# FFN up-projection tiles: three 256-column matmuls per weight tile, or one of 512 and one of 256 columns with the halves added afterwards

## Chip, cores and metric

The kernel runs on one core of a Trainium2 chip. The metric is the device time of one execution in microseconds (us); the time before is the median of three runs. Engines are named as in the profile: PE (TensorE, matmuls), PEld (its weight loads), DVE (VectorE), ACT (ScalarE), SP (the queue that issues the DMAs).

## Reference

Two decoder layers on a sequence of 256 tokens with 1024 channels, float32. Layer 0 is FFN, pool/SSD mixer, FFN; layer 1 is FFN, latent attention, FFN. Every sub-layer takes a normed and modulated input h. The part that the change touches is the FFN, which occurs four times:

```
def swiglu(h, w13, w2):
    a, b = jnp.split(h @ w13, 2, axis=-1)
    return (jax.nn.silu(a) * b) @ w2
```

h is 256 x 1024, w13 is 1024 x 5632 (2816 columns for a, 2816 for b), w2 is 2816 x 1024. The four FFNs are called FFN0 and FFN1 (layer 0), FFN2 and FFN3 (layer 1) below. The vectors that scale, shift and gate each sub-layer come from another product, c @ mod_w, spread over the kernel.

## The kernel before

Channels lie on the 128 partitions and the 256 tokens along the free dimension. Matmuls run in a reduced float32 format, so every float32 operand is split into a high part (rounded) and a low part (the rest), and a product is the sum of three: weight low x input high, weight high x input low, weight high x input high.

**Weights.** SP loads blocks of 16 weight tiles (128 x 128 each, 1 MB) into `raw` buffers. Half a block, a piece of 8 tiles, is rounded by ACT into `wh` (L222), and DVE subtracts to get `wl` (L223). The function `take()` hands out pieces in the order in which the matmuls use them and writes the preparation of a piece into the program four pieces ahead; `wh` and `wl` have five buffers each, so a piece can be prepared only when the tile five pieces earlier has been used. Between the weight blocks stand blocks of mod_w, two DVE instructions each (L210), which multiply and sum for the vectors of later sub-layers. FFN0 has one such block for nearly every weight block, FFN1 and FFN2 one for every second.

**An FFN** has two stages. In the a/b stage each of 22 column tiles j makes a pair: a_j and b_j, each 8 steps over the 1024 channels (one piece per tile). Then ACT computes s = silu(a) (L589), DVE g = b * s (L590), and `split` rounds g on ACT (L314) and takes the rest on DVE (L315), giving the high and low halves of column tile j. In the f stage eight output tiles f_d run over all 22 column tiles of g, and DVE adds each to x through the gate (L446, two instructions); from the new x, `chunk` makes the next sub-layer's input parts `uh` (ACT, L375) and `ul` (DVE, L376). The next sub-layer begins with matmuls named `u_...` that use these parts one channel tile after another, the last tile last.

**Two forms of a step.** The f stage and the output projections use `mm2`: the input lies as high and low half side by side (512 columns), `wh` meets both in one matmul, and `wl` meets the high half in a second one that adds onto one half of the result. The two halves of the result are added later (in the f stage by the two L446). The a/b stage uses `mm3` through `lin`: three matmuls of 256 columns onto one 256-column result. The input `hx` already lies side by side.

**What is not touched.** The first 8 pairs of FFN0 come from a special start (tiles `n`), and the first 3 pairs of FFN1, FFN2 and FFN3 from `norm.open` (tiles `u_a`, `u_b`). So `lin` makes 14 pairs in FFN0 (j = 8 to 21) and 19 in each other FFN (j = 3 to 21): 71 pairs, 142 tiles.

The order of each engine's instructions is fixed when the program is built, by a scheduler with its own estimates; on the chip each engine goes through its list strictly in order.

Of the kernel before, what the change touches and what calls it, by code (L numbers as in the profile page):

```python
# [13 lines left out]
AF = mybir.ActivationFunctionType  # L14
ALU = mybir.AluOpType
# [4 lines left out]
S = 256  # L20
NC = D // P
# [40 lines left out]
def trunk(ctx, tc, xT, c_row, pos, kc, cols, rows, mod_w, w13s, w13, w2, win_a, wdt,  # L62
          pool_w, wout_a, win_m, wkr, wkv, wq, wo, out):
    nc = tc.nc
    V, A, T = nc.vector, nc.scalar, nc.tensor
# [9 lines left out]
    def ps(name):  # L75
        return pp.tile([P, 512], F32, tag="ps", name=name)
# [3 lines left out]
    def slab(q, name, dt, shape):  # L80
        n = int(np.prod(shape))
        t = ap_.tile([P, n], dt, tag=f"s{q}", name=name)
        if len(shape) == 1:
            return t
        names = "abc"[: len(shape)]
        spec = f"p ({' '.join(names)}) -> p {' '.join(names)}"
        return t.rearrange(spec, **dict(zip(names, shape)))

    def tmp(name):
        return tp.tile([P, S], F32, tag="t", name=name)  # L90
# [154 lines left out]
    def take(m=1):  # L245
        if cur["off"] == 0:
            while len(pieces) < cur["piece"] + state["look"] and process_half():
                pass
        wh, wl, n = pieces[cur["piece"]]
        o = cur["off"]  # L250
        cur["off"] += m
        assert cur["off"] <= n
        if cur["off"] == n:
            cur["piece"] += 1
            cur["off"] = 0
        return wh[:, o * P : (o + m) * P], wl[:, o * P : (o + m) * P]

    def mm3(pt, w, xh, xl, first, last):
        wh, wl = w
        T.matmul(pt, wl, xh, start=first, stop=False)  # L260
        T.matmul(pt, wh, xl, start=False, stop=False)  # L261
        T.matmul(pt, wh, xh, start=False, stop=last)  # L262

    def mm2(pt, w, x, first, last):
        wh, wl = w
        T.matmul(pt, wh, x, start=first, stop=False)  # L266
        T.matmul(pt[:, S:], wl, x[:, 0], start=False, stop=last)  # L267
# [28 lines left out]
    def prep_gate(l, sub):  # L296
        i = l * 3 + sub
        m, b = mod_col(l, 3 * sub + 2)
        V.tensor_tensor(out=gt_t[:, i], in0=m, in1=b, op=ALU.add)
        if sub != 1:  # L300
            V.tensor_scalar(out=gt_t[:, i], in0=gt_t[:, i], scalar1=0.5, scalar2=None, op0=ALU.mult)
        return gt_t[:, i]
# [3 lines left out]
    hx = cp.tile([P, NC, 2, S], F32R, name="hx")  # L306
# [6 lines left out]
    def split(dh, dl, src):  # L313
        A.copy(dh, src)  # L314
        V.tensor_tensor(out=dl, in0=src, in1=dh.bitcast(F32), op=ALU.subtract)  # L315
# [37 lines left out]
    def warm_sqrt(name):  # L353
        d = sp.tile([P, 1], F32, tag="wsq", name=f"wsq_{name}", bufs=1)
        A.activation(d, eps_t, AF.Sqrt)
# [74 lines left out]
    def lin(name, xh, xl, nk=NC):  # L430
        pt = ps(name)
        for k in range(nk):
            mm3(pt[:, :S], take(), xh(k), xl(k), k == 0, k == nk - 1)
        return pt

    def lin2(name, x, nk):
        pt = ps(name)
        for k in range(nk):
            mm2(pt, take(), x(k), k == 0, k == nk - 1)
        return pt  # L440

    hhk, hlk = (lambda k: hh[:, k]), (lambda k: hl[:, k])

    def residual(pt, d, gate, nxt):
        for e in range(2):
            V.scalar_tensor_tensor(out=xt[:, d], in0=pt[:, e * S : (e + 1) * S], scalar=gate[:, d : d + 1],  # L446
                                   in1=xt[:, d], op0=ALU.mult, op1=ALU.add)
        nxt.chunk(d)
# [109 lines left out]
    def ffn(norm, l, sub, make_next, opened=()):  # L558
        gt = [slab(q, f"g{l}{sub}_{q}", F32R, [2, 2, S]) for q in range(NSLAB)]

        def gx(j):
            return gt[j // 2][:, j % 2]

        for j in range(NJ):
            s = tmp(f"s{l}{sub}{j}")
            g = tmp(f"g{l}{sub}{j}")
            if not opened and j < NU:
                pa, pb = norm.open((f"a{j}", f"b{j}"))
                if j == 0:
                    norm.finish()  # L570
                r = norm.r
                ba = sp.tile([P, 1], F32, tag="ub", name="ba")
                V.tensor_copy(ba, pa[:, S : S + 1])
                ta, tb = tmp("ta"), tmp("tb")
                V.tensor_tensor(out=ta, in0=pa[:, :S], in1=r, op=ALU.mult)
                A.activation(s, ta, AF.Silu, bias=ba[:, 0:1])
                V.tensor_tensor(out=tb, in0=pb[:, :S], in1=r, op=ALU.mult)
                V.scalar_tensor_tensor(out=g, in0=tb, scalar=pb[:, S : S + 1], in1=s,
                                       op0=ALU.add, op1=ALU.mult)
                for c in range(8):  # L580
                    if c * NU // 8 == j:
                        norm.h(c)
            else:
                if 2 * j < len(opened):
                    pa, pb = opened[2 * j : 2 * j + 2]
                else:
                    pa = lin(f"a{j}", hhk, hlk)
                    pb = lin(f"b{j}", hhk, hlk)
                A.activation(s, pa[:, :S], AF.Silu)  # L589
                V.tensor_tensor(out=g, in0=pb[:, :S], in1=s, op=ALU.mult)  # L590
            split(gx(j)[:, 0], gx(j)[:, 1], g)
        gate = prep_gate(l, sub)
        nxt = make_next()
        if (l, sub) == (1, 0):
            rope_tables()
        warm_sqrt(f"f{l}{sub}")
        for d in range(NC):
            pt = lin2(f"f{d}", gx, NJ)
            residual(pt, d, gate, nxt)
        return nxt  # L600
# [294 lines left out]
    def rope_tables():  # L895
        ang = tmp("ang")
        posi = tp.tile([P, S], I32, tag="t", name="posi")
        nc.sync.dma_start(posi, pos.partition_broadcast(P))
        V.tensor_copy(ang, posi)
        V.tensor_scalar(out=ang, in0=ang, scalar1=kct[:, KC_INV : KC_INV + 1], scalar2=None, op0=ALU.mult)  # L900
        for dst, shift in ((sin_t, 0.0), (cos_t, 0.25)):
            n = tmp("angn")
            t = tmp("angt")
            V.tensor_scalar(out=n, in0=ang, scalar1=float(1.0 / TWO_PI), scalar2=shift, op0=ALU.mult, op1=ALU.add)
            V.tensor_scalar(out=n, in0=n, scalar1=MAGIC, scalar2=None, op0=ALU.add)
            V.tensor_scalar(out=n, in0=n, scalar1=-MAGIC, scalar2=None, op0=ALU.add)
            V.scalar_tensor_tensor(out=t, in0=n, scalar=-C1, in1=ang, op0=ALU.mult, op1=ALU.add)
            V.scalar_tensor_tensor(out=t, in0=n, scalar=-C2, in1=t, op0=ALU.mult, op1=ALU.add)
            V.scalar_tensor_tensor(out=t, in0=n, scalar=-C3, in1=t, op0=ALU.mult, op1=ALU.add)
            if shift:  # L910
                V.tensor_scalar(out=t, in0=t, scalar1=float(np.pi / 2), scalar2=None, op0=ALU.add)
            V.tensor_scalar(out=t, in0=t, scalar1=PI_IN, scalar2=-PI_IN, op0=ALU.min, op1=ALU.max)
            A.activation(dst, t, AF.Sin)
# [269 lines left out]
    n = Norm(0, 0, scaled=False)  # L1183
    with tc.manual_schedule(engines={mybir.EngineType.PE, mybir.EngineType.DVE, mybir.EngineType.Activation}):
        pts = first_pairs(n)
    state["pin"] = True
    n = ffn(n, 0, 0, lambda: Norm(0, 1), pts)
    n = mixer_ab(n, 0, lambda: Norm(0, 2))
    n = ffn(n, 0, 2, lambda: Norm(1, 0))
    n = ffn(n, 1, 0, lambda: Norm(1, 1))  # L1190
    n = mixer_mla(n, 1, lambda: Norm(1, 2))
    n = ffn(n, 1, 2, Final)
# [144 lines left out]
```

## Time and profile before

| what | value |
|---|---|
| median of three runs | 1041.67 us (1041.18 to 1043.35) |
| profiled execution: its time, its span | 1042.6 us, 1040.8 us |
| busy in the span: PE, PEld, DVE, ACT | 1022.4, 957.7, 844.2, 576.4 us |
| granted TensorE clock, mean over the span | 0.993 |
| DMA, mean | 245 GB/s |

The span is the stretch that the trace covers; the execution's own time is 1.8 us longer. A busy PE row counts matmuls whose ends are modelled, so the pace of PE is read from start to start of successive matmuls and not from the duration of one. A name in brackets behind an instruction's idle time is what ended that wait.

### The profile page before, as it was taken

The page shows a single profiled execution, that of the slowest core. Times are in us where ns is not written, and L with a number is a line of the kernel's source. Part 1 is how long each engine was busy: PE and PEld are TensorE (multiplying, and loading weights), DVE is VectorE, ACT ScalarE, POOL GpSimd, SP SyncE. Part 2 cuts the span into 40 slices and gives each one's busy share as a digit, 9 for nine tenths or more (in the row PEclk, how much of TensorE's full clock was granted, in tenths as well). Part 3 has the DMA queues.
Part 4 walks back from the last instruction along what each step waited for, and adds up shares of the span by engine and source line. Part 5 has one row for each costly group of instructions (what it writes and reads, how often), then busy time and mean ns, then how long its engine had stood idle before and what let it go on. Part 6 is the DMA issues. An engine that isn't in the chain of part 4 may idle for free.

```text
span 1040.8 us, 18493 instructions
## 1 busy us (share of the span) xinstructions
PE 1022.4 (98%) x7436; PEld 957.7 (92%) x7436; DVE 844.2 (81%) x1523; ACT 576.4 (55%) x982; POOL 0.2 (0%) x4
## 2 busy tenths in 40 slices
PE   9899999999999999999999999999999999999997
PEld 7899998899878999998899999989988799999986
DVE  6888989999999887778879777899888688666553
ACT  3474453468795654445456444454678665444542
POOL 0000000000000000000000000000000000000000
PEclk9899999999999999999999999999999999999999
DMA  9988988977534477778766777798643246656501
GB/s 352 395 306 330 364 300 340 346 276 266 202 143 154 170 285 281 248 283 326 283 237 228 270 289 273 244 356 310 240 174 115 77 162 246 241 207 240 174 30 41
DMA packets 38648, 255.06 MB, mean 245 GB/s; under 512 B 4241, under 2 KB 6817, under 8 KB 8738
## 3 DMA queue, kind: packets, MB, share of 16 engines
q1 hardware_dynamic: 38562, 253.88, 66.6%
q8 instruction: 58, 0.95, 0.4%
q14 instruction: 28, 0.23, 0.1%
HBM read 252.79 MB, written 1.06 MB: 244 GB/s over the span
## 4 chain that ended last, share of the span: by engine, by line
PE 87%; DVE 7%; ACT 3%; DMA 1%; issue 1%; SPq 0%; DVEq 0%; ACTq 0%
PE f L266 15%; PE f L267 8%; PE a L260 7%; PE b L261 7%; PE b L260 7%; PE b L262 7%; PE a L262 7%; PE a L261 7%; PE o L266 4%; DVE wl L223 3%; DVE raw L210 2%; PE o L267 2%; PE n L522 1%; PE s L1074 1%; DMA raw<-in_w13s 1%; PE u_a L260 1%
## 5 line engine op out<-in xcount | busy, mean ns | idle before, releaser
L223 DVE TENSOR_TENSOR wl<-raw,wh 128x1024 fp32r<-128x1024 f32 x327 | 396.7, 1220 | 123.9 <-ACT wh L222 116.5
L222 ACT CAST wh<-raw 128x1024 fp32r<-128x1024 f32 x327 | 338.8, 1047 | 220.9 <-issue 92.9
L266 PE MATMUL f<-g,wh 128*128 128x512 f32 x704 | 248.9, 399 | 0.0
L267 PE MATMUL f<-g,wl 128*128 128x256 f32 x704 | 197.7, 281 | 0.0
L210 DVE SCALAR_TENSOR_TENSOR raw<-raw,c_bc 128x1024 f32<-128x1024 f32 x144 | 173.2, 1218 | 0.8 <-DMA raw<-in_mod_w 0.7
L266 PEld LDWEIGHTS f<-g,wh 128*128 128x128 f32 x704 | 132.3, 188 | 32.8
L260 PE MATMUL a<-hx,wl 128*128 128x256 f32 x568 | 160.8, 283 | 0.0
L261 PE MATMUL b<-hx,wh 128*128 128x256 f32 x568 | 160.7, 283 | 0.0
L262 PE MATMUL b<-hx,wh 128*128 128x256 f32 x568 | 160.7, 283 | 0.0
L260 PE MATMUL b<-hx,wl 128*128 128x256 f32 x568 | 160.7, 283 | 0.0
L262 PE MATMUL a<-hx,wh 128*128 128x256 f32 x568 | 160.6, 283 | 0.0
L261 PE MATMUL a<-hx,wh 128*128 128x256 f32 x568 | 160.5, 283 | 0.0
L267 PEld LDWEIGHTS f<-g,wl 128*128 128x128 f32 x704 | 133.0, 189 | 0.0
L260 PEld LDWEIGHTS a<-hx,wl 128*128 128x128 f32 x568 | 109.0, 192 | 0.6 <-ACT hx L400 0.6
L261 PEld LDWEIGHTS b<-hx,wh 128*128 128x128 f32 x568 | 109.1, 192 | 0.0
L262 PEld LDWEIGHTS b<-hx,wh 128*128 128x128 f32 x568 | 109.1, 192 | 0.0
L260 PEld LDWEIGHTS b<-hx,wl 128*128 128x128 f32 x568 | 109.0, 192 | 0.0
L262 PEld LDWEIGHTS a<-hx,wh 128*128 128x128 f32 x568 | 109.0, 192 | 0.0
L261 PEld LDWEIGHTS a<-hx,wh 128*128 128x128 f32 x568 | 108.9, 192 | 0.0
L589 ACT ACTIVATE s<-a 128x256 f32<-128x256 f32 x71 | 27.3, 384 | 88.5 <-PE a L262 88.5
L314 ACT CAST g<-g 128x256 fp32r<-128x256 f32 x88 | 35.3, 404 | 28.6 <-DVE g L590 19.8
L266 PE MATMUL o<-hx,wh 128*128 128x512 f32 x128 | 47.2, 410 | 0.7 <-DVE hx L315 0.7
(397 smaller groups left out, 1701.2 us busy)
## 6 DMA issues: line engine op xcount, KB each, us to landing
raw<-in_w SPq DMA_DIRECT2D x124, 1024.0 KB, 5.0
raw<-in_mod_w SPq DMA_DIRECT2D x70, 1024.0 KB, 5.3
raw<-in_win_a SPq DMA_DIRECT2D x12, 1024.0 KB, 7.1
raw<-in_w13s SPq DMA_DIRECT2D x7, 1024.0 KB, 11.1
raw<-in_wout_a SPq DMA_DIRECT2D x6, 1024.0 KB, 5.5
raw<-in_wq SPq DMA_DIRECT2D x5, 1024.0 KB, 4.8
raw<-in_win_m SPq DMA_DIRECT2D x4, 1024.0 KB, 5.0
raw<-in_wo SPq DMA_DIRECT2D x4, 1024.0 KB, 5.5
```

What stands on the lines that cost most here:

```text
L210: V.scalar_tensor_tensor(out=sl, in0=sl, scalar=1.0, in1=c_bc, op0=ALU.mult, op1=ALU.mult, accum_out=modc[:, c0 : c0 + 1])
L222: A.copy(wh[:, :n], src)
L223: V.tensor_tensor(out=wl[:, :n], in0=src, in1=wh[:, :n].bitcast(F32), op=ALU.subtract)
L260: T.matmul(pt, wl, xh, start=first, stop=False)
L261: T.matmul(pt, wh, xl, start=False, stop=False)
L262: T.matmul(pt, wh, xh, start=False, stop=last)
L266: T.matmul(pt, wh, x, start=first, stop=False)
L267: T.matmul(pt[:, S:], wl, x[:, 0], start=False, stop=last)
L314: A.copy(dh, src)
L522: T.matmul(tile_of(m), w, x[:, k], start=k == 0 and m % 2 == 0 and w is wl, stop=k == NC - 1 and w is wh and x is hh, skip_group_check=True)
L589: A.activation(s, pa[:, :S], AF.Silu)
L1074: T.matmul(pts[e][:, lo : lo + n], q[:, lo : lo + P], kk[:, 0:n], start=True, stop=False)
```

## The change

The a and b tiles that `lin` made are now made by `lin2`, with `mm2`: per step one 512-column matmul of `wh` with both halves of `hx`, and one 256-column matmul of `wl` with the high half, whose product lands on the second half of the result. The two halves have to be added before silu and before the product, so for each tile ACT copies the second half out of PSUM into a new buffer `ta` or `tb`, and DVE adds the first half to it. Silu and the product then read these buffers instead of PSUM. The count of matmuls falls from 24 to 16 a tile, the count of columns stays (768 a step); 142 copies and 142 additions are new.

```diff
                 if 2 * j < len(opened):
-                    pa, pb = opened[2 * j : 2 * j + 2]
+                    pa, pb = (p[:, :S] for p in opened[2 * j : 2 * j + 2])
                 else:
-                    pa = lin(f"a{j}", hhk, hlk)
-                    pb = lin(f"b{j}", hhk, hlk)
-                A.activation(s, pa[:, :S], AF.Silu)
-                V.tensor_tensor(out=g, in0=pb[:, :S], in1=s, op=ALU.mult)
+                    pa, pb = tmp("ta"), tmp("tb")
+                    for n, p in (("a", pa), ("b", pb)):
+                        pt = lin2(f"{n}{j}", lambda k: hx[:, k], NC)
+                        A.copy(p, pt[:, S:])
+                        V.tensor_tensor(out=p, in0=pt[:, :S], in1=p, op=ALU.add)
+                A.activation(s, pa, AF.Silu)
+                V.tensor_tensor(out=g, in0=pb, in1=s, op=ALU.mult)
```

All lines below the insertion stand three further down in the changed kernel: L589 and L590 become L592 and L593, and L590 and L591 are now the copy and the addition.

**DVE in FFN0, around pair 14.** Names: `g0014` is g of layer 0, FFN0, column tile 14; `wl34_0` and `wl34_1` are the two pieces of one weight block; `raw..., modc` is a mod_w block. Before, from the end of pair 13 to the end of pair 14:

```order
L315 TENSOR_TENSOR g00_6_725<-g0013_1127,g00_6_725 128x256
L223 TENSOR_TENSOR wl32_0_1235<-raw32_1088,wh32_0_1234 128x1024
L223 TENSOR_TENSOR wl32_1_1270<-raw32_1088,wh32_1_1269 128x1024
L210 SCALAR_TENSOR_TENSOR raw33_1092,modc_84<-raw33_1092,c_bc_75 128x1024
L590 TENSOR_TENSOR g0014_1197<-b14_1227,s0014_1196 128x256
L210 SCALAR_TENSOR_TENSOR raw33_1092,modc_84<-raw33_1092,c_bc_75 128x1024
L315 TENSOR_TENSOR g00_7_726<-g0014_1197,g00_7_726 128x256
```

In the changed kernel, the same stretch:

```order
L315 TENSOR_TENSOR g00_6_725<-g0013_1077,g00_6_725 128x256
L591 TENSOR_TENSOR ta_1138<-a14_1140,ta_1138 128x256
L210 SCALAR_TENSOR_TENSOR raw31_988,modc_84<-raw31_988,c_bc_75 128x1024 x2
L591 TENSOR_TENSOR tb_1139<-b14_1163,tb_1139 128x256
L223 TENSOR_TENSOR wl34_0_1231<-raw34_1104,wh34_0_1230 128x1024
L593 TENSOR_TENSOR g0014_1137<-tb_1139,s0014_1136 128x256
L223 TENSOR_TENSOR wl34_1_1262<-raw34_1104,wh34_1_1261 128x1024
L315 TENSOR_TENSOR g00_7_726<-g0014_1137,g00_7_726 128x256
```

Two additions are new in each pair, and the two mod_w instructions now stand between them.

**ACT in FFN0, pairs 13 and 14.** Before, from silu of pair 13 to the rounding of g of pair 14:

```order
L589 ACTIVATE s0013_1126<-a13_1128 128x256
L222 CAST wh30_1_1199<-raw30_1018 128x1024
L222 CAST wh32_0_1234<-raw32_1088 128x1024
L314 CAST g00_6_725<-g0013_1127 128x256
L589 ACTIVATE s0014_1196<-a14_1198 128x256
L222 CAST wh32_1_1269<-raw32_1088 128x1024
L314 CAST g00_7_726<-g0014_1197 128x256
```

In the changed kernel, from silu of pair 13 to silu of pair 14:

```order
L592 ACTIVATE s0013_1076<-ta_1078 128x256
L222 CAST wh32_0_1170<-raw32_1044 128x1024
L222 CAST wh32_1_1201<-raw32_1044 128x1024
L590 COPY ta_1138<-a14_1140 128x256
L590 COPY tb_1139<-b14_1163 128x256
L314 CAST g00_6_725<-g0013_1077 128x256
L592 ACTIVATE s0014_1136<-ta_1138 128x256
```

The rounding of g of pair 13 stood ahead of everything of pair 14 before; now it stands behind the copies of a14 and b14.

**ACT in FFN1, pairs 8 and 9, in the changed kernel** (`g028` is g of column tile 8, `a9` the a tile of the next pair):

```order
L590 COPY tb_4290<-b8_4314 128x256
L592 ACTIVATE s028_4287<-ta_4289 128x256
L222 CAST wh101_1_4408<-raw101_4199 128x1024
L314 CAST g02_4_3732<-g028_4288 128x256
L590 COPY ta_4345<-a9_4347 128x256
L222 CAST wh102_0_4433<-raw102_4255 128x1024
```

Here the rounding of g stands ahead of the copies of the next pair, in some other pairs of FFN1 behind the copy of the next a.

## Rows read from the trace of the kernel before

**Rows 1.** The page, busy time by engine: us, share, instructions.
```profile
PE 1022.4 (98%) x7436; PEld 957.7 (92%) x7436; DVE 844.2 (81%) x1523; ACT 576.4 (55%) x982; POOL 0.2 (0%) x4
```

**Rows 2.** The page, chain that ended last, shares of the span by engine.
```profile
PE 87%; DVE 7%; ACT 3%; DMA 1%; issue 1%; SPq 0%; DVEq 0%; ACTq 0%
```

**Rows 3.** Windows by stage: length, then busy us (instructions) per engine, PEclk, DMA.
```profile
69.63:150.26 80.63, 80.63 (x674) 80.63 (x673) 69.87 (x109) 39.89 (x60) 0.00 (x0) 1.00 0.88 323
150.50:212.46 61.96, 61.96 (x352) 53.71 (x351) 59.08 (x97) 26.69 (x37) 0.00 (x0) 1.00 0.89 333
360.40:469.86 109.46, 109.46 (x912) 109.26 (x911) 85.40 (x132) 56.28 (x86) 0.00 (x0) 1.00 0.75 275
550.00:659.50 109.50, 109.50 (x913) 109.30 (x913) 86.89 (x135) 54.97 (x84) 0.00 (x0) 1.00 0.76 275
860.50:969.96 109.46, 109.46 (x913) 109.26 (x912) 74.59 (x110) 55.64 (x86) 0.00 (x0) 1.00 0.63 230
```

**Rows 4.** Groups by line and shape: xcount | busy us, mean ns | idle before.
```profile
L260 PE MATMUL a<-hx,wl 128*128 128x256 f32 x568 | 160.8, 283 | 0.0
...
L260 PE MATMUL b<-hx,wl 128*128 128x256 f32 x568 | 160.7, 283 | 0.0
```

**Rows 5.** Timeline of PE in FFN1's a/b stage: start us, us, what.
```profile
400.74 0.28 PE L260 MATMUL a<-hx,wl 128*128 128x256 f32 x1
...
403.62 0.28 PE L260 MATMUL b<-hx,wl 128*128 128x256 f32 x1
```

**Rows 6.** Timeline of PE in FFN1's f stage.
```profile
469.86 0.40 PE L266 MATMUL f<-g,wh 128*128 128x512 f32 x1
...
473.39 0.40 PE L266 MATMUL f<-g,wh 128*128 128x512 f32 x1
```

**Rows 7.** Timeline of PE in the first mixer's output projection.
```profile
324.43 0.39 PE L266 MATMUL o<-hx,wh 128*128 128x512 f32 x1
...
325.81 0.39 PE L266 MATMUL o<-hx,wh 128*128 128x512 f32 x1
```

**Rows 8.** Timeline of DVE in FFN0's a/b stage, one pair, [idle before <-releaser].
```profile
110.91 0.42 DVE L590 TENSOR_TENSOR g<-b,s 128x256 f32<-128x256 f32 x1
111.25 1.22 DVE L210 SCALAR_TENSOR_TENSOR raw<-raw,c_bc 128x1024 f32<-128x1024 f32 x1
...
112.39 0.42 DVE L315 TENSOR_TENSOR g<-g,g 128x256 fp32r<-128x256 f32 x1
112.76 1.23 DVE L223 TENSOR_TENSOR wl<-raw,wh 128x1024 fp32r<-128x1024 f32 x1
114.38 1.23 DVE L223 TENSOR_TENSOR wl<-raw,wh 128x1024 fp32r<-128x1024 f32 x1 [0.40 <-ACT wh L222]
115.53 1.22 DVE L210 SCALAR_TENSOR_TENSOR raw<-raw,c_bc 128x1024 f32<-128x1024 f32 x1
...
116.67 0.42 DVE L590 TENSOR_TENSOR g<-b,s 128x256 f32<-128x256 f32 x1
```

**Rows 9.** Timeline of ACT: a copy of a matmul result, 128x256.
```profile
286.55 0.37 ACT L672 COPY bc<-z 128x256 f32<-128x256 f32 x1 [1.73 <-PE z L262]
```

**Rows 10.** Groups by line: the rounding of g, the product on DVE.
```profile
L314 ACT CAST g<-g 128x256 fp32r<-128x256 f32 x88 | 35.3, 404 | 28.6 <-DVE g L590 19.8 <-DVE g L578 6.1
...
L590 DVE TENSOR_TENSOR g<-b,s 128x256 f32<-128x256 f32 x71 | 30.0, 422 | 9.5 <-PE b L262 9.5
```

**Rows 11.** Timeline of DVE in FFN0's f stage.
```profile
158.24 1.00 DVE L446 SCALAR_TENSOR_TENSOR xt<-f,gt_t,xt 128x256 f32<-128x256 f32 x2 [0.85 <-PE f L267]
...
200.84 0.49 DVE L376 SCALAR_TENSOR_TENSOR ul<-xt,gs_t,uh 128x256 fp32r<-128x256 f32 x1 [0.58 <-ACT uh L375]
```

**Rows 12.** Timeline of PE at the end of FFN0.
```profile
212.34 0.28 PE L267 MATMUL f<-g,wl 128*128 128x256 f32 x1
212.46 0.28 PE L260 MATMUL u_B<-uh,wl 128*128 128x258 f32 x1
...
218.62 0.39 PE L261 MATMUL u_B<-ul,wh 128*128 128x258 f32 x1 [0.70 <-DVE ul L376]
```

## The prediction

> **What bounds the kernel now.** I read the page first: PE is busy 98% of the span, DVE 81% and ACT 55% [rows 1], and 87% of the chain that ended last lies on PE [rows 2]. A busy PE alone does not say that PE sets the pace, so I cut the FFNs into stages [rows 3]. In every a/b stage PE is busy for the whole stretch at a granted clock of 1.00, that is at the 2.4 GHz level, and DVE is not: 69.87 of 80.63 us in FFN0, 85.40 of 109.46 in FFN1, 86.89 of 109.50 in FFN2, 74.59 of 109.46 in FFN3. So a faster PE shortens these stages, as long as DVE can follow. FFN0 is the place to look at: DVE is busy 87% in its a/b stage and 59.08 of 61.96 us in its f stage, and at its end PE does wait 0.70 us for DVE's `ul` of the last channel tile [rows 12]. There the next sub-layer's start hangs on DVE, not on PE.
>
> **The change on PE.** `lin` made 568 steps for a and 568 for b [rows 4], 1136 steps in 142 tiles. A tile's eight steps of three matmuls take 403.62 - 400.74 = 2.88 us, 0.360 us a step [rows 5]. The new form of a step stands in the f stage: from the first to the eleventh 512-column matmul, ten steps, 473.39 - 469.86 = 3.53 us, 0.353 a step [rows 6]. That is 0.0067 us a step (0.360 less 0.3533; the f stages hold this value over all their steps), 0.053 a tile. The nearest other row is the output projection, which reads the very buffer `hx`: four steps in 325.81 - 324.43 = 1.38 us, 0.345 a step [rows 7]. I take 0.3533, because the f stages have by far the most such steps; 0.345 would make it 0.015 a step and is the far bound; no gain at all is the near bound, since the columns a step stay 768. PE's gain is 28 tiles x 0.053 = 1.49 us in FFN0 and 38 x 0.053 = 2.03 in each other FFN, 7.6 in all.
>
> The Trainium skill, TensorE: Matmul & The Clock Gate, section Back-to-back issue gap, gives the gap of isolated matmuls as columns over 2.4 GHz plus 2.5 ns. An estimate by it is 0.3275 us for the old step and 0.325 for the new, 2.5 ns saved a step and 2.3 us instead of 6.1 in FFN1 to FFN3, which would make the sum below 1040.4 us. The trace differs from it, with 0.360 and 0.353 [rows 5, 6], and the measurement decides.
>
> **The change on ACT.** 142 copies out of PSUM. A copy of this shape takes 0.37 us [rows 9]: 2 x 0.37 = 0.74 more a pair, 14.1 in an FFN of 19 pairs. ACT then has some 70 of 107 us there [rows 3], so the copies cost nothing by their own time; what hides them is ACT's idle time between PE's tiles. What they do to the order comes below.
>
> **The change on DVE.** 142 additions. The nearest instruction is the product g = b * s, one PSUM operand and one in SBUF, 0.422 us long [rows 10], but what it takes of DVE's time behind another instruction is start to start: 111.25 - 110.91 = 0.34 us [rows 8]. A long one (`wl` or mod_w) takes 1.14 to 1.15. I take 0.34 for an addition; the upper bound is 0.34 plus a full hand-over from ACT, for which DVE waits 0.58 where it has nothing to put in between [rows 11].
>
> In FFN1 and FFN2 DVE comes to 85.4 + 38 x 0.34 = 98.3 and 99.8 us of 107.4, in FFN3 to 87.5. DVE still has room, and a piece may be ready four pieces ahead, so PE keeps its pace: -2.03 us each, -6.1 in all.
>
> In FFN0 the account is another. A pair with a mod_w block now takes 116.67 - 110.91 = 5.76 us, of which DVE is idle 0.40 before a `wl` and the rest is four long and two short instructions, 4 x 1.145 + 2 x 0.34 = 5.26 [rows 8]. With two additions it is 5.94, while PE's pair falls to 16 x 0.3533 = 5.65. So DVE becomes the slower one by 0.29 a pair, and 11 of the 12 pairs from the tenth on have such a block. How late it gets I follow from the order of pair 13: its last `split` waits for ACT's rounding, which stands behind the copy of b14. b14 ends at 69.63 + 14 tiles x 2.827 = 109.2, plus 0.16 for the last matmul's remaining length, 0.37 for the copy and 0.40 for the rounding [rows 3, 5, 9, 10]: 110.1. From there to the f stage's first `xt` DVE's list holds 32 long and 33 short instructions and four tiny ones (estimate 0.15 each): 36.6 + 11.2 + 0.6 = 48.5, so that `xt` starts at 158.6. Before, it started at 158.24 after a wait of 0.85 for PE [rows 11]. Three more tiny ones, 0.55, which were done before that `xt`, now follow it. So DVE is about 1.0 us later from here on, and from here to the last `ul` its list is the same as before and nearly without idle time: 59.08 busy of 61.96, and what is idle is the hand-over to ACT, which stays [rows 3, 11]. The last `ul`, for which PE waited until 218.62 [rows 12], then lets it go on at 219.6: FFN0 ends 1.0 us later than before, although PE needs 1.5 less. PE's gain there turns into a longer wait, 0.7 + 1.5 + 1.0 = 3.2 us, part of it already inside the f stage when a `wl` is late.
>
> Everything behind (both mixers, the f stages, the final norm) keeps its instructions. Sum: -6.1 + 1.0 = -5.1 us. The profiled execution's own 1042.6 us would become 1037.5; the median of the runs shown lies 0.9 lower, so the forecast is 1036.6 us.
>
> **Rivals.**
> 1. *DVE is not late in FFN0.* If the additions disappear in its idle time (10.8 us in the a/b stage, and 24 x 0.34 = 8.2 is less than that), FFN0 gains its 1.49 too: 1041.67 - 7.6 = 1034.1. For it: the totals fit. Against it: DVE's idle time of the first pairs and the wait before pair 13's `split` cannot be stored. A pace of 0.345 a step would add to this: -17 us at the most over all 1136 steps, against which the f stages speak.
> 2. *PE gains next to nothing.* If the step is paid by columns, 768 before and after, the a/b step stays at 0.360: 1041.67 + 1.0 = 1042.7. Against it: the f step has the same 768 columns and takes 0.353 [rows 6]. The Trainium skill's page TensorE: Matmul & The Clock Gate (Back-to-back issue gap), comes near this rival with the 1040.4 us estimated by it above.
> 3. *Slower: DVE waits for ACT at each addition.* If every addition in FFN0 finds its copy not done, it costs 0.58 more [rows 11]; 24 of them are 13.9 us on an engine that is already the bound: 1036.6 + 13.9 = 1050.5. It turns the whole to slower by over 0.2% from 0.30 us an addition on (7.2 us). For it: ACT's list holds the copies behind roundings that wait for DVE. Against it: in DVE's order two mod_w instructions, 2.29 us, stand between the two additions, and a late DVE finds the copies done. The Trainium skill, Perfetto Trace Analysis, section Optimizing Scalar/DVE Operations, speaks against the change: each instruction pays a fixed access time, about 125 ns for DVE on PSUM, and on a saturated engine one should group work into larger operations. The trace agrees in kind: 256 columns take 0.34 us and 1024 take 1.145, so 1.05 ns a column and 0.07 fixed [rows 8]. With the page's 0.125 instead, an estimate, an addition takes 0.39 and FFN0's 24 end 1.3 us later, 1037.9 in all.
>
> **How the numbers follow.** The forecast 0.60, rival 1 0.14, rival 2 0.14, rival 3 0.12. A measurement of this kernel tells about 0.2%, 2.1 us, from no change: below 1039.6 is faster, above 1043.8 slower. Forecast and rival 1 are faster, 0.74; rival 2 is the same, 0.14; rival 3 is slower, 0.12. The range leaves out rival 3, the upper part of rival 2 and the far bound of the step: 1033.0 to 1040.6. The forecast's own range, with an addition at 0.34 to 0.42 in FFN0 (24 x 0.08 = 1.9 later) or DVE 1 us less late, is 1035.5 to 1038.6.
>
> **What would show it.** In the profile after: an a tile in 2.82 to 2.84 us from start to start; the a/b stages of FFN1 to FFN3 2 us shorter each with no new wait on PE; in FFN0 DVE near fully busy from about 110 us to the end of its f stage, PE waiting there for `wl` or `ul` 2 to 4 us in all, and the mixer's `u_B` going on at about 219.6. It would be wrong if PE's step in the a/b stage were not 0.353, if DVE waited on ACT's copies in FFN1 to FFN3 until `wl` came late, or if FFN0's end moved by more than 2 us from there.

## The result and the profile after

The changed kernel takes 1029.61 us in the median of four runs (1028.05 to 1032.29), the kernel before 1041.82 beside it: a ratio of 0.9887, 95% interval 0.9875 to 0.9899. That is 11.8 us less by the ratio, where 5.1 were predicted. The direction was right, the size was outside the range (1033.0 to 1040.6). The profiled execution has a span of 1030.5 us, 10.3 less than before.

The page after, busy time by engine (answers to [rows 1]): PE stays at 98% with 1136 matmuls fewer, DVE rises from 81% to 86%, ACT from 55% to 60%.

```profile
PE 1010.1 (98%) x6300; PEld 895.1 (87%) x6300; DVE 887.4 (86%) x1665; ACT 617.6 (60%) x1124; POOL 0.2 (0%) x4
```

The windows by stage (columns as in [rows 3]): FFN0's a/b and f stage, then the a/b stages of FFN1, FFN2 and FFN3, each of these from its first step in the new form to the first f step.

```profile
69.46:148.62 79.16, 79.16 (x451) 68.68 (x450) 74.76 (x130) 45.03 (x82) 0.00 (x0) 1.00 0.85 305
148.62:211.77 63.15, 62.03 (x354) 53.52 (x353) 60.44 (x101) 28.04 (x41) 0.00 (x0) 1.00 0.94 347
362.73:468.35 105.62, 105.62 (x611) 92.19 (x609) 95.83 (x166) 65.69 (x120) 0.00 (x0) 1.00 0.78 278
547.11:652.75 105.64, 105.64 (x611) 92.22 (x610) 96.08 (x167) 65.69 (x120) 0.00 (x0) 1.00 0.78 278
852.35:959.63 107.28, 107.28 (x610) 93.14 (x609) 87.69 (x148) 65.17 (x120) 0.00 (x0) 1.00 0.67 235
```

FFN0's a/b stage is 1.47 us shorter than in [rows 3], as predicted (1.49). But FFN1 and FFN2 lose 3.85 us each against the windows there (4.0 against a window cut in the same way, below), twice the predicted 2.03. FFN3 loses 2.2 to 2.4, near to it. So the same 38 tiles, of the same instructions, ran at two paces, at a granted clock of 1.00 in both. The timeline of PE shows them: an a tile of FFN1 and one of FFN3, each with the first step of the b tile that follows.

```profile
401.79 0.40 PE L266 MATMUL a<-hx,wh 128*128 128x512 f32 x1
...
404.56 0.40 PE L266 MATMUL b<-hx,wh 128*128 128x512 f32 x1
...
880.48 0.40 PE L266 MATMUL a<-hx,wh 128*128 128x512 f32 x1
...
883.31 0.40 PE L266 MATMUL b<-hx,wh 128*128 128x512 f32 x1
```

Eight steps take 2.77 us in FFN1 and 2.83 in FFN3, with no wait in either; as means over longer stretches that is 0.3467 and 0.3533 us a step. The f stages changed too, though their instructions are those of before. In FFN1's, eleven long matmuls span ten steps:

```profile
473.20 0.40 PE L266 MATMUL f<-g,wh 128*128 128x512 f32 x1
...
476.67 0.40 PE L266 MATMUL f<-g,wh 128*128 128x512 f32 x1
```

That is 3.47 us, where [rows 6] have 3.53. In this execution FFN0's a/b stage and FFN3 run at 0.3533, and most of what has that form from inside FFN0's f stage to the end of FFN2 at 0.3467; the exceptions are the first steps of a stage and the steps around waits.

The end of FFN0, on PE's timeline, came out as predicted: PE goes on at 219.61 (forecast 219.6, before 218.62 in [rows 12]). So the 1.47 us of the a/b stage do not shorten the kernel: PE waits that much longer.

```profile
217.49 0.50 PE L260 MATMUL u_B<-uh,wl 128*128 128x258 f32 x2 [0.42 <-ACT uh L375]
219.61 0.39 PE L261 MATMUL u_B<-ul,wh 128*128 128x258 f32 x1 [1.62 <-DVE ul L376]
```

What follows this wait was not foreseen. Two windows, the second of them around the wait and the first right behind it: PE, idle for half of 216 to 220, then has a granted clock of 0.57, near the 1.2 GHz level.

```profile
220.00:224.00 4.00, 4.00 (x21) 3.83 (x21) 3.81 (x6) 2.30 (x3) 0.00 (x0) 0.57 1.00 356
216.00:220.00 4.00, 1.96 (x14) 1.54 (x14) 4.00 (x8) 1.75 (x3) 0.00 (x0) 1.00 0.96 354
```

It does 21 matmuls in 4 us where it did 34 in the second profiled execution (below): about 1.5 us lost. By the starts of the stages FFN1 and FFN2 give 5.2 us each in a/b and f together, FFN3 2.4, and FFN0 with the stretch at 1.2 GHz takes 2.5 back: 10.3, the difference of the spans.

### The profile page after: what moved, and what is told of

Its sections match the earlier page's. It is cut to its first block, busy times and chain, and to the rows that moved or that the text cites. A ratio compares the mean times of both kernels' runs of the same rounds, so it can differ in the third digit from the quotient of the medians.

```text
span 1030.5 us, 16634 instructions
## 1 busy us (share of the span) xinstructions
PE 1010.1 (98%) x6300; PEld 895.1 (87%) x6300; DVE 887.4 (86%) x1665; ACT 617.6 (60%) x1124; POOL 0.2 (0%) x4
## 4 chain that ended last, share of the span: by engine, by line
PE 85%; DVE 9%; ACT 3%; DMA 1%; issue 1%; SPq 0%; DVEq 0%; ACTq 0%
PE f L266 14%; PE a L266 13%; PE b L266 13%; PE f L267 7%; PE a L267 6%; PE b L267 6%; PE o L266 4%; DVE wl L223 3%; DVE raw L210 3%; PE o L267 2%; PE n L522 1%; PE s L1077 1%; DMA raw<-in_w13s 1%; PE u_a L260 1%; PE u_b L261 1%; PE u_a L261 1%
## 5 line engine op out<-in xcount | busy, mean ns | idle before, releaser
L266 PE MATMUL f<-g,wh 128*128 128x512 f32 x704 | 245.7, 395 | 0.0
L266 PE MATMUL a<-hx,wh 128*128 128x512 f32 x568 | 202.9, 396 | 0.0
L266 PE MATMUL b<-hx,wh 128*128 128x512 f32 x568 | 202.7, 396 | 0.0
L266 PEld LDWEIGHTS b<-hx,wh 128*128 128x128 f32 x568 | 106.6, 188 | 25.3
L266 PEld LDWEIGHTS a<-hx,wh 128*128 128x128 f32 x568 | 106.6, 188 | 25.3 <-DVE hx L401 0.3
L375 ACT ACTIVATE uh<-xt,gs_t 128x256 fp32r<-128x256 f32 x40 | 20.3, 507 | 43.5 <-DVE xt L446 43.4
L522 PE MATMUL n<-hx,wh 128*128 128x256 f32 x224 | 41.9, 289 | 0.0
L446 DVE SCALAR_TENSOR_TENSOR xt<-f,gt_t,xt 128x256 f32<-128x256 f32 x64 | 30.7, 480 | 12.7 <-PE f L267 12.4
L315 DVE TENSOR_TENSOR g<-g,g 128x256 fp32r<-128x256 f32 x88 | 36.6, 418 | 1.9 <-ACT g L314 1.9
L522 PE MATMUL n<-hx,wl 128*128 128x256 f32 x112 | 32.9, 294 | 4.8 <-DVE wl L223 4.8
## 6 DMA issues: line engine op xcount, KB each, us to landing
raw<-in_w SPq DMA_DIRECT2D x124, 1024.0 KB, 5.0
raw<-in_mod_w SPq DMA_DIRECT2D x70, 1024.0 KB, 5.1
raw<-in_win_a SPq DMA_DIRECT2D x12, 1024.0 KB, 7.0
raw<-in_w13s SPq DMA_DIRECT2D x7, 1024.0 KB, 10.2
raw<-in_wout_a SPq DMA_DIRECT2D x6, 1024.0 KB, 4.7
raw<-in_wq SPq DMA_DIRECT2D x5, 1024.0 KB, 5.2
raw<-in_win_m SPq DMA_DIRECT2D x4, 1024.0 KB, 5.2
raw<-in_wo SPq DMA_DIRECT2D x4, 1024.0 KB, 4.8
```

The lines of the kernel that those rows point to most:

```text
L375: A.activation(uh[:, c, :S], x, AF.Identity, bias=0.0, scale=g)
L522: T.matmul(tile_of(m), w, x[:, k], start=k == 0 and m % 2 == 0 and w is wl, stop=k == NC - 1 and w is wh and x is hh, skip_group_check=True)
```

## Experiments

My first theory was that the pace of the step hangs on the order in which PE gets long (512-column) and short (256-column) matmuls. The scheduler mixes two tiles at some places, so that two long ones stand in a row and then two short ones. The timeline of the changed kernel shows such a place in FFN0's f stage (x2: two in a row, drawn from the start of the first):

```profile
155.67 0.40 PE L266 MATMUL f<-g,wh 128*128 128x512 f32 x1
...
156.38 0.63 PE L266 MATMUL f<-g,wh 128*128 128x512 f32 x2
156.85 0.39 PE L267 MATMUL f<-g,wl 128*128 128x256 f32 x2
157.08 0.40 PE L266 MATMUL f<-g,wh 128*128 128x512 f32 x1
157.31 0.28 PE L267 MATMUL f<-g,wl 128*128 128x256 f32 x1
157.43 0.39 PE L266 MATMUL f<-g,wh 128*128 128x512 f32 x1
```

Ahead of it two steps take 0.71 us (155.67 to 156.38) and the pace is 0.3533; behind it the pace is 0.3467. The rivals were that the pace is chance, or a property of the a/b form.

**again.** The changed kernel once more, unchanged.

> The changed kernel as it is. In its first profile the step of a 512-column and a 256-column matmul ran at two paces: 0.3533 us in FFN0's a/b stage and in FFN3, 0.3467 us from inside FFN0's f stage to the end of FFN2. Order theory (the pace hangs on the order in which the program issues long and short matmuls, and on PE's waits): the same paces in the same stages again, span within 2 us of 1030.5. Rival (the pace is chance, drawn anew in each execution): other stages at other paces.

1030.69 us median (1025.78 to 1032.18), ratio 0.9886 (0.9869 to 0.9904). The profiled execution has a span of only 1024.0, where 1030.5 within 2 us was expected. FFN0 to FFN2 show the same paces at the same places, but FFN3 now runs at 0.3467, and the stretch behind FFN0's end stays at the 2.4 GHz level after the same wait:

```profile
848.78:954.27 105.49, 105.49 (x611) 92.92 (x609) 87.52 (x148) 65.12 (x120) 0.00 (x0) 1.00 0.69 239
220.00:224.00 4.00, 4.00 (x34) 3.95 (x33) 3.97 (x7) 2.30 (x3) 0.00 (x0) 1.00 0.99 311
```

So both theories are half right: most places repeat, FFN3 does not. These two differences, and a stretch near 1.2 GHz at 312 to 320 us which this execution lacks and the profiled ones of both kernels first shown have, account for about 6 of the 6.5 us between the two spans (FFN3 3.0, the stretches 1.5 and 1.6).

**pinned.** PE's steps of a, b and f strictly tile after tile.

```diff
+            at = len(nc.cur_bb.bb.instructions)
             mm2(pt, take(), x(k), k == 0, k == nk - 1)
+            for ins in nc.cur_bb.bb.instructions[at:]:
+                if isinstance(ins, mybir.InstMatmult):
+                    if state.get("mm"):
+                        tc.add_manual_dep(ins, state["mm"], ORDER, reason="tile order")
+                    state["mm"] = ins.name
```

> The changed kernel with the 512+256-column steps of a, b and f issued strictly tile after tile; the scheduler's mixing of two tiles, by which two long matmuls stand in a row and then two short ones, is gone. Order theory: nothing shifts the alternation, a/b and f stages of FFN1 and FFN2 run at 0.3533 us, 3.2 us an FFN longer than in the changed kernel, so about 1029.6 + 6.4 = 1036. Rival (the quick pace comes from what the a/b stage is made of, or from chance): 0.3467 stays, 1029 to 1031.

1053.49 us (ratio 1.0113, 1.0097 to 1.0129): neither theory. FFN0 ran at 0.3533 in both stages, its f stage too, which has no mixing now. FFN1 to FFN3 ran at 0.3467 all the same. They began with waits of PE, two in each, which the mixing had filled; the view of waits gives their sum, their count and the longest:

```profile
PE a L266 <- DVE hx L401: 14.1, 6, 3.1
```

So mixing is not needed for the better pace. A wait of PE ahead of the stream may bring it as well; no run has such waits as its only change. The time itself is that of the waits and of stretches of a lower granted clock behind them (0.52 at 872 to 876 us).

**before_swap.** The kernel before, with a shift put in by hand in each f stage (`lin2` with `swap`, set for the second f tile).

```diff
...
+        if swap:
+            p = [(take(), x(k)) for k in (0, 1)]
+            for i in (0, 1):
+                T.matmul(pt, p[i][0][0], p[i][1], start=i == 0, stop=False)
+            for i in (1, 0):
+                T.matmul(pt[:, S:], p[i][0][1], p[i][1][:, 0], start=False, stop=False)
+            ks = ks[2:]
...
```

> The kernel before with one edit: in the second f tile of each FFN the first two steps are issued long, long, short, short. Order theory: from there the f stage runs at 0.3467 instead of 0.3533 us, 154 steps x 0.0066 = 1.0 us in each of FFN1 to FFN3 (FFN0's end hangs on DVE), so 3.0 us less: about 1038.8. Rival (order does not set the pace): f stages at 0.3533, 1041.8.

1039.08 us, ratio 0.9972 (0.996 to 0.9983), 2.9 us less than before by the ratio, where 3.0 were expected. The timeline of FFN1's f stage shows ten steps of 3.53 us ahead of the swapped pair and ten of 3.47 behind it, where nothing but an order was changed:

```profile
474.03 0.40 PE L266 MATMUL f<-g,wh 128*128 128x512 f32 x1
...
477.56 0.40 PE L266 MATMUL f<-g,wh 128*128 128x512 f32 x1
...
478.62 0.40 PE L266 MATMUL f<-g,wh 128*128 128x512 f32 x1
...
482.09 0.40 PE L266 MATMUL f<-g,wh 128*128 128x512 f32 x1
```

All four f stages change over at that place. The lists of DVE and ACT are those of before, and PE's differs in these few matmuls alone. This settles that the pace can be set by order alone.

**late3.** The change in FFN1 to FFN3 only; FFN0 as before.

```diff
...
+                elif (l, sub) == (0, 0):
+                    pa = lin(f"a{j}", hhk, hlk)[:, :S]
+                    pb = lin(f"b{j}", hhk, hlk)[:, :S]
...
```

> The change in FFN1 to FFN3 alone; FFN0 keeps three matmuls a step and has no copies and additions. If the loss of FFN0 and the start of the first mixer (2.5 us in the traces) comes from DVE's additions in FFN0, it is gone and FFN1 to FFN3 gain as in the changed kernel: 1029.6 - 2.5 = 1027.1. If the quick pace of FFN1 and FFN2 were inherited from FFN0's f stage, they would run at 0.3533 and the time would be about 1027.1 + 6.4 = 1033.5.

1027.93 us, ratio 0.9862 (0.9848 to 0.9875). FFN0's loss is gone. Its f stage ran at 0.3533 and FFN1 and FFN2 at 0.3467, so their pace was not inherited from FFN0.

**late3_swap.** The same with `swap` at two tiles: a12 of FFN1 and a6 of FFN3.

> The change in FFN1 to FFN3 alone, and two tiles begin with long, long, short, short: a12 of FFN1, where the step was at 0.3467 us, and a6 of FFN3, where it was at 0.3467 in two profiles and at 0.3533 in one. If such a pair always ends in the quick pace: FFN1 stays at 0.3467, FFN3 is at 0.3467 in every execution, 1025 to 1027. If it only shifts, and so can also end the quick pace: FFN1 at 0.3533 from a12 on, 336 steps x 0.0066 = 2.2 us more, and FFN3 perhaps too.

1030.22 us, ratio 0.9884 (0.9867 to 0.9901). FFN1 went from 0.3467 to 0.3533 at a12. Its timeline ahead of the swapped pair (ten steps in 3.46 us) and behind it (ten in 3.54):

```profile
406.01 0.39 PE L266 MATMUL a<-hx,wh 128*128 128x512 f32 x1
...
409.47 0.39 PE L266 MATMUL b<-hx,wh 128*128 128x512 f32 x1
...
410.51 0.63 PE L442 MATMUL a<-hx,wh 128*128 128x512 f32 x2
...
411.20 0.40 PE L266 MATMUL a<-hx,wh 128*128 128x512 f32 x1
...
414.74 0.40 PE L266 MATMUL b<-hx,wh 128*128 128x512 f32 x1
```

FFN3 stayed at 0.3467. So the swapped pair can end the better pace as well as begin it, and in FFN3 it changed nothing.

**ffn0, mm2_alone, adds_alone** ask what the copies and additions cost. The first has the change in FFN0 only (the branch of late3 with `!=`). The second makes the new matmuls, and leaves out the other half of the result:

```diff
...
+                    pa = lin2(f"a{j}", lambda k: hx[:, k], NC)[:, :S]
+                    pb = lin2(f"b{j}", lambda k: hx[:, k], NC)[:, :S]
...
```

The third keeps three matmuls a step and adds the copies and as many DVE instructions of that size:

```diff
...
+                        pt = lin(f"{n}{j}", hhk, hlk)
+                        A.copy(p, pt[:, :S])
+                        V.tensor_tensor(out=p, in0=pt[:, :S], in1=p, op=ALU.max)
...
```

> The change in FFN0 alone; FFN1 to FFN3 keep three matmuls a step. If the prediction's account of FFN0 holds (DVE becomes the bound there, FFN0 ends about 1.0 us later although PE needs less), the time is 1041.4 + 0.9 = 1042.3, and up to 1043.8 in executions where PE's longer wait at FFN0's end is followed by a stretch at the 1.2 GHz level, as in the first profile of the changed kernel. Rival 1 (DVE not late in FFN0): 1039.9.

> Leaves out the second half: a and b are the first 256 columns alone, without the low input's product, so no copies and no additions; PE's steps are those of the change. If copies and additions cost nothing in FFN1 to FFN3, this gains there what the change in FFN1 to FFN3 alone gains, and FFN0's end still hangs on DVE as before: 1026 to 1028.6. Rival (they cost PE time there too): the change in FFN1 to FFN3 alone, 1027.9, is slower than this by over 2 us.

> Three matmuls a step as before, with copies and DVE instructions of the same kind and size as the change's (the larger of the result and its copy, which is the result). The prediction's account: nothing in FFN1 to FFN3; in FFN0 DVE's 24 extra instructions of 0.34 us make its pair 5.94 us against PE's 5.76, so FFN0 ends 1.0 us later and up to 0.75 more because PE is slower ahead of pair 13: 1042.4 to 1043.2, plus 1.5 in executions with a stretch at 1.2 GHz behind the wait. Rival (DVE waits for ACT at every addition): 10 us and more.

ffn0: 1044.58 us, ratio 1.0028 (1.0017 to 1.0038): a loss of 2.9, where 0.9 to 2.4 was expected. Its profiled execution was the shortest of the eight, with no stretch at 1.2 GHz behind FFN0's end, so what the others lose more is not shown. mm2_alone: 1027.6, ratio 0.9874 (0.9859 to 0.9889), no faster than late3, which has copies and additions. That these are free in FFN1 to FFN3 is read from the windows, as mm2_alone has other losses in FFN0. FFN1's a/b stage in mm2_alone, late3 and adds_alone:

```profile
361.34:466.98 105.64, 105.64 (x611) 92.20 (x610) 86.97 (x134) 56.63 (x85) 0.00 (x0) 1.00 0.77 285
```

```profile
361.03:466.67 105.64, 105.64 (x610) 92.16 (x609) 95.88 (x166) 65.70 (x120) 0.00 (x0) 1.00 0.79 279
```

```profile
361.23:470.90 109.67, 109.67 (x914) 109.47 (x913) 98.59 (x168) 64.94 (x120) 0.00 (x0) 1.00 0.73 268
```

The first two agree to the hundredth with 9 us of DVE work between them. The third is the length of before: three matmuls a step, whatever DVE does. But adds_alone was a miss in FFN0: 1041.59 us, ratio 1.0 (0.9991 to 1.0009). All 28 additional instructions of FFN0 were there, and FFN0 ended only 0.06 us later, counted from its first a step. So the additions themselves do not make FFN0 late. Nor are they needed for it: mm2_alone, without any, ends FFN0 1.2 us late as well, with two waits of 1.48 us for PE in DVE's f stage. DVE's waits in the changed kernel tell more: from pair 13 to its first addition to the residual it has two, both for ACT's rounding of g. The later one, 1.30 us, is 0.21 in adds_alone. ACT's timeline at the end of FFN0's a/b stage, then DVE's two waits and the first addition to the residual, then the wait in adds_alone:

```profile
146.60 0.36 ACT L590 COPY ta<-a 128x256 f32<-128x256 f32 x1
148.82 0.37 ACT L590 COPY tb<-b 128x256 f32<-128x256 f32 x1 [1.86 <-PE b L267]
149.09 0.41 ACT L314 CAST g<-g 128x256 fp32r<-128x256 f32 x1
```

```profile
109.95 0.42 DVE L315 TENSOR_TENSOR g<-g,g 128x256 fp32r<-128x256 f32 x1 [0.38 <-ACT g L314]
...
149.53 0.43 DVE L315 TENSOR_TENSOR g<-g,g 128x256 fp32r<-128x256 f32 x1 [1.30 <-ACT g L314]
...
159.19 0.48 DVE L446 SCALAR_TENSOR_TENSOR xt<-f,gt_t,xt 128x256 f32<-128x256 f32 x1
```

```profile
149.04 0.43 DVE L315 TENSOR_TENSOR g<-g,g 128x256 fp32r<-128x256 f32 x1 [0.21 <-ACT g L314]
```

The copy of b21 stands in ACT's list ahead of the rounding of g20. It waits for PE's last a/b matmul; the rounding, long possible, waits behind it, and DVE, which sets the pace from here to FFN0's last `ul`, stands idle for 1.30. At pair 13 the rounding stands behind the copy of b14 in the same way, for 0.38.

**round_first, swap0, both** test that. round_first orders each b copy of FFN0 behind the previous rounding:

```diff
...
                         A.copy(p, pt[:, S:])
+                        if (l, sub, n) == (0, 0, "b"):
+                            tc.add_manual_dep(nc.cur_bb.bb.instructions[-1], state["round"], ORDER,
+                                              reason="rounding first")
...
-            split(gx(j)[:, 0], gx(j)[:, 1], g)
+            A.copy(gx(j)[:, 0], g)
+            state["round"] = nc.cur_bb.bb.instructions[-1].name
...
```

swap0 sets `swap` for FFN0's first a tile, both does the two.

> The changed kernel, with ACT's copy of each b tile in FFN0 ordered behind the rounding of the previous pair's g. In the changed kernel the copy of b21, which waits for PE's last a/b matmul of FFN0, stands ahead of the rounding of g20, and DVE waits 1.30 us for it; its first addition to the residual comes 89.7 us after FFN0's first a/b step, 88.6 in the kernel before. Queue theory (this place in ACT's list sets how late FFN0 ends): 88.6 again, PE goes on 1.1 us earlier behind FFN0's last low part, time 1.1 us below the changed kernel's 1030, and up to 1.5 more where the stretch at 1.2 GHz behind that wait goes too. Rival (the prediction's: the length of DVE's own list from pair 13 on): 89.7 stays.

> The changed kernel, where FFN0's first a tile begins long, long, short, short, to bring FFN0's a/b stage from 0.3533 to 0.3467 us a step: PE would end that stage 224 x 0.0066 = 1.5 us earlier. Queue theory: DVE's wait for the rounding behind the copy of b21 shrinks from 1.30, FFN0 ends up to 1.1 us earlier, 1029. Rival (the prediction's: DVE's own list is the bound): FFN0 ends when it did, PE waits 1.5 us longer, 1030.

> Both edits together: the copy of b tiles behind the previous rounding in FFN0, and FFN0's first a tile begun long, long, short, short. Queue theory: DVE's list is then the bound of FFN0 and one edit takes all that is to be had, so the same as the rounding alone, about 1029. Rival: the two add up, 2 us and more below the changed kernel.

round_first: 1026.33 us, ratio 0.9864 (0.9848 to 0.988), the lowest median of all, though its interval overlaps that of late3 and, at its end, that of the changed kernel. Both waits, 0.38 and 1.30, are gone. ACT's rounding comes at 147.40, ahead of the copy, and DVE's first addition to the residual 87.9 us after FFN0's first step at 69.53 (89.7 in the changed kernel, so 1.9 earlier where 1.1 was expected, and 0.7 earlier than in the kernel before, with all additions in place); PE goes on at 217.83 behind the same wait:

```profile
147.40 0.41 ACT L597 CAST g<-g 128x256 fp32r<-128x256 f32 x1
148.88 0.37 ACT L590 COPY tb<-b 128x256 f32<-128x256 f32 x1 [1.07 <-PE b L267]
```

```profile
157.40 0.48 DVE L446 SCALAR_TENSOR_TENSOR xt<-f,gt_t,xt 128x256 f32<-128x256 f32 x1
```

```profile
217.83 0.39 PE L261 MATMUL u_B<-ul,wh 128*128 128x258 f32 x1 [1.61 <-DVE ul L376]
```

swap0: 1030.42 us, ratio 0.9891 (0.9872 to 0.991), so no gain to be told in the time. Its profile shows what the queue theory said: FFN0's a/b stage at 0.3467, DVE's wait down to 0.51 us, the residual's first addition 1.5 us earlier. It shows one thing more. FFN0's f stage has the same mixed place as in the changed kernel, in the same order, but here it ends the better pace: ten steps of 3.47 us ahead of it, ten of 3.53 behind.

```profile
151.07 0.39 PE L266 MATMUL f<-g,wh 128*128 128x512 f32 x1
...
154.54 0.39 PE L266 MATMUL f<-g,wh 128*128 128x512 f32 x1
154.88 0.63 PE L266 MATMUL f<-g,wh 128*128 128x512 f32 x2
155.58 0.40 PE L266 MATMUL f<-g,wh 128*128 128x512 f32 x1
...
159.11 0.40 PE L266 MATMUL f<-g,wh 128*128 128x512 f32 x1
```

All six profiles with the change in FFN0 and this mixed place shift there: after, again, ffn0 and round_first to 0.3467, swap0 and both to 0.3533. pinned and mm2_alone, which lack the place, go on at 0.3533 through it.

both: 1027.92, ratio 0.9876 (0.9859 to 0.9894); FFN0's residual begins 0.25 us earlier than with the rounding alone, so the edits do not add up. In its profile FFN1 and FFN2 run at 0.3533, behind the same order of PE as in swap0, where they ran at 0.3467.

## Why the prediction was wrong

The direction, the bound and most steps held. The step that failed is the price of the new form, "I take 0.3533, because the f stages have by far the most such steps", and with it "Everything behind (both mixers, the f stages, the final norm) keeps its instructions", taken to mean that it keeps its time.

- **PE's gain a step (mis-sized).** Predicted 0.360 - 0.3533 = 0.0067 us. In FFN1 and FFN2 it was 0.360 - 0.3467 = 0.0133, that is 304 steps x 0.0133 = 4.0 us a stage, and 176 f steps x 0.0066 = 1.2 on top: 5.2 each instead of 2.03. [Rows 7] showed this pace, 0.345, in the kernel before. I kept it as a bound and gave it no chance of its own; what tells it from 0.3533 (rows of the same form, no waits, two paces) was in the trace and was not followed up. The range ended where only a part of it fitted in. In the spans the sum then closes: they differ by 10.3, 5.2 more than the predicted 5.1, and of this FFN1 and FFN2 give 6.37 and FFN3 0.36, while FFN0 with the stretch behind its end takes 1.54 back.
- **Which pace.** before_swap shows that an order of four matmuls can set it, pinned suggests that waits do it too, late3_swap and the mixed place in FFN0's f stage that a shift can go either way. What decides which pace follows a shift was not settled: FFN3 differs between executions of one program, and FFN1 and FFN2 between swap0 and both.
- **FFN0 (right size by luck, wrong reason).** Predicted: 1.0 us late through DVE's longer list from pair 13 on. Measured: PE goes on at 219.61, 0.99 later than before. DVE's list from pair 13's last `split` to the first addition to the residual starts at 109.95 where 110.1 was forecast, and takes 47.9 us without its wait, where 48.5 was counted. Without the 1.30 us wait behind the copy of b21 that addition would stand at 157.89, which is 88.43 us after FFN0's first a step; the kernel before has 88.61. So the list alone made nothing late (adds_alone), and the term is the wait (round_first), which the sum did not have. This is near to rival 3, DVE waiting for ACT, but at a rounding and not at the additions. The order behind it was read only at pair 13. Rival 1 spoke truer of the additions: DVE's idle time did absorb them.
- **Copies and additions free in FFN1 to FFN3.** Held: 105.64 us with and without.
- **Rival 2** (no gain for PE) fell at once: the new step is below 0.360 at both paces. The Trainium skill, TensorE: Matmul & The Clock Gate, section Back-to-back issue gap, gives the gap of isolated matmuls, and an estimate by it makes the new step 0.325 us and the saving 2.5 ns. The runs have 0.3467 and 0.3533, and the measurement decides.
- **The stretch at 1.2 GHz** behind FFN0's longer wait, 1.5 us in the first profile and none in the second, was no term of the sum at all.

## What to carry to other kernels

When one form of instruction shows two paces without waits in the trace of before, price the change by both, with a chance for each, and look at what stands where one turns into the other. An in-order engine that is 60% busy can still cost time: look in its list for an instruction that waits for the bottleneck ahead of one for which the second-busiest engine is waiting, and order the two. Where such a pair decides, reorder it before giving up the change there: with the rounding put first, PE went on behind FFN0 0.7 us earlier than in the kernel before, counted from FFN0's first a step, and not 1.2 later. In the time this is not told apart from leaving FFN0 as it was (late3).

## What the runs showed of the hardware

Each matmul that is dropped from an a/b step, at equal columns, saved 0.0133 us in the better pace (three in 0.360 us, two in 0.3467), at a granted clock of 1.00. In the other pace the steps take 0.350, 0.349 and 0.361 in turn, where the better has 0.343 and 0.350. In the places looked at, the pace changed only where the stream was broken by another order, another form or a wait, and it held for 100 us and more in between. The same two long and two short matmuls in FFN0's f stage turned 0.3533 into 0.3467 in the changed kernel and 0.3467 into 0.3533 in swap0. The same PE wait of about 2 us was followed by the 1.2 GHz level in one execution of the changed kernel and by 2.4 GHz in another.
